# One channel tile at a time in the plain projections, and a third PSUM bank for neighbourhood outputs

## The chip, the core and the metric

The kernel runs on one core of a Trainium2 chip. The metric is device time in microseconds (us); lower is better. A core has a matrix engine (TensorE, PE in the profile, with its weight loads as PEld), VectorE (DVE), ScalarE (ACT), GpSimd (POOL) and SyncE (SP), which here issues nearly all DMA transfers, one after the other from one queue. [...] TensorE is throttled at times: the profile gives its granted clock, 1.00 being full speed.

## What is computed

One layer of an encoder over a prompt of 1024 tokens and a sample of 256, width 2048, then a final norm:

```python
hn = rmsnorm(x, norm_w)
proj = jnp.einsum('btd,dp->btp', hn, w_in)
cuts = [int(c) for c in np.cumsum([NA_WIDTH] * 4 + [2 * ML_WIDTH, ML_WIDTH, ML_WIDTH, ML_WIDTH])]
na_q, na_k, na_v, na_g, ml_qk, ml_v, ml_o, ml_z, ml_gp = jnp.split(proj, cuts, axis=-1)
...
att = (att * jax.nn.silu(na_g)).astype(x.dtype)
qk = jax.nn.silu(centred_depthwise_conv(ml_qk, conv_w, conv_b))
...
h = bidirectional_mlstm(mq, mk, mv, gates)
h = rmsnorm(h, head_norm_w.reshape(ML_HEADS, ML_HEAD_DIM)).reshape(B, T, ML_WIDTH)
mem = (h * jax.nn.sigmoid(ml_o.astype(f32)) * jax.nn.silu(ml_z.astype(f32))).astype(x.dtype)
mixed = jnp.concatenate([att, mem], axis=-1)
return x + jnp.einsum('btm,md->btd', mixed, w_out)
```

`att` is neighbourhood attention: 8 heads of width 128, each token attending to a window of 8 x 16 tokens in a grid 64 wide, with a learned bias. The mLSTM has 4 heads of width 256 and runs over chunks in both directions. The sample and the prompt are separate sequences. Everything is float32; the kernel splits each operand into a high and a low part and adds three products (high-high, high-low, low-high).

## The kernel before, in words

**Stages.** Channels of the projection come in tiles of 128, numbered from `QT0` (attention q), `KT0` (k), `GT0` (gates), `QK0` (the mLSTM's q and k, with a convolution), `OT0` and `ZT0` (its gates); v comes in units `u` of `proj_v`. First comes group A of the tokens (768 of the prompt), in `pair_a` with Strassen-like sums, to about 1097 us. Then group B (the last 256 of the prompt and the sample, 512 tokens): some pairs of tiles by `pair_s` (those in `SECOND`), the others plainly by `proj_pair` and `proj_v`. From about 1350 us attention and the mLSTM run beside these plain units, to about 2115 us; then the pairs of `late_gate`, and from 2160 us the output projection (`product`, L1613), with weights loaded from `w_o` into tiles `wr_wp` (pieces of 512 KB through the ring of `w_piece`), `wb` and `T`, split into `wo`.

**What sets the order.** All loops are unrolled by a planner that simulates the program and gives every engine a fixed order; each engine then waits on semaphores. The function `run` (L1304) issues two streams at high priority: the units of attention (`na_sample`, then `na_prompt` with its four blocks, for each of 8 heads) and those of the mLSTM (tiles `mls`, `mlp`). The plain projection units are of normal priority and fill TensorE where the streams cannot. DMAs go out of SP's queue in program order, each when its own waits are met, so a waiting DMA holds those behind it.

**PSUM.** `bank` (L73) gives a tile of one bank from one of two rings: `pr`, three banks, for the projections, and `a`, five banks, for everything else (scores, transposes, outputs of attention, the mLSTM's sums). `first_tiles`, `pair_a`, `pair_s` and the output projection (`p_banks`) take from both.

**`proj_pair` (L650).** A pair of channel tiles takes two `pr` banks. For each of four weight pieces (`w_piece`, 512 KB, a ring of two) it splits the columns of both tiles (`w_split`, ACT writes the high part at L165, DVE the low at L166), and goes through the four 128-column blocks of each split, for each of which the three products of the two tiles follow one another; 96 matmuls of 128 x 512 in all (`pc`, L662). Then both tiles are evicted (`out_scaled`, L251) and stored.

**`proj_v` (L709 on).** A unit of v takes two `pr` banks with two token tiles of 256 columns each (`pv`, L740), all four of which are evicted at the end by `store_v` (L221): ACT writes the high part (L168), DVE the low (L169) of a tile `vo`, which is stored to DRAM (`vS`).

**`na_sample` (L795) and `na_prompt` (L837).** Each loads q and k from DRAM (`qS`, `kS`), 2 x 256 KB for the sample and 2 x 1024 KB for the prompt, into a tile `qk` of tag `nqk`, which has one buffer. `na_softmax` computes scores into a bank `s` (L773) and the softmax, `na_transpose` the transposes (L790), and the products with v go to a bank `o` of ring `a`. The mLSTM's q, k, v tiles come from a ring `hf` of eight buffers.

**Square of the hidden state (L1258 to 1259).** Its value `jk` is not used, only its row sums; it goes into a ring `sml` of six small tiles.

## Time and profile before

| | us |
|---|---|
| median of 3 runs | 2563.29 |
| lowest, highest | 2563.03, 2566.54 |
| profiled execution | 2565.18 |
| its span | 2563.3 |

The mean granted clock of the profiled execution is 0.997. The page gives busy time, share of the span and number of instructions for each engine, and the chain of work that ended last, followed back from the last instruction. The rows of waits read: engine, what it ran next, its line, what released it; then total us, times and the longest one. A row of windows gives busy time of PE, PEld, DVE, ACT and POOL with the number of instructions, the granted clock, the DMA share and GB/s. In rows of a tile, three figures with slashes are the minimum, median and maximum duration in ns. Chain rows are start, duration, and what.

The span falls into these stages:

| us | stage |
|---|---|
| 7 to 1097 | projections of group A |
| 1097 to 1350 | first units of group B, pairs of `SECOND` |
| 1350 to 2115 | attention and mLSTM, plain units between |
| 2113 to 2153 | last pairs of `late_gate` |
| 2160 to 2554 | output projection |

### The profile page before, as it was taken

To read this page: it belongs to the slowest core of one execution; us is meant where nothing else is said; L and a number is where in the kernel's file an instruction comes from. 1 tells how busy PE (TensorE), PEld (TensorE's weight loads), DVE (VectorE), ACT (ScalarE), POOL (GpSimd) and SP (SyncE) were. 2 spreads that over 40 slices of the span, in tenths; PEclk is the share of its full clock that TensorE was granted. 3 is DMA by queue.
4 is the path that set the end of the run, shared out by engine and by line. 5 is a ranking of instruction groups with operands and counts; after the bars stand their busy time and mean duration, and the time that the engine had idled before them with its cause. 6 is when DMAs were issued, how large, how long until landed. Compare 5 with 4: busy or idle time off the path is not lost.

```text
span 2563.3 us, 44540 instructions
## 1 busy us (share of the span) xinstructions
PE 2534.0 (99%) x15054; PEld 2368.6 (92%) x15054; DVE 1972.6 (77%) x4029; ACT 1345.0 (52%) x3041; POOL 615.3 (24%) x909
## 2 busy tenths in 40 slices
PE   8999999999999999999999999999999999999998
PEld 8999999999999999999999999998988887788886
DVE  8769888888869798898875866765855665879695
ACT  8535545444444444465655666655745543344444
POOL 0535555444544444410001110100100104000001
PEclk9999999999999999999999999999999999999999
DMA  6546464536434342467768878877867849636237
GB/s 215 174 143 200 143 199 130 179 124 200 125 112 126 101 141 89 154 228 223 239 223 299 297 243 272 293 234 261 286 197 251 277 126 377 202 125 218 85 87 254
DMA packets 303483, 503.03 MB, mean 196 GB/s; under 512 B 48752, under 2 KB 191256, under 8 KB 303256
## 3 DMA queue, kind: packets, MB, share of 16 engines
q1 hardware_dynamic: 299096, 484.46, 58.9%
q0 software_dynamic: 4160, 15.73, 1.6%
q8 instruction: 119, 1.95, 0.3%
q14 instruction: 108, 0.88, 0.1%
HBM read 373.13 MB, written 126.95 MB: 195 GB/s over the span
## 4 chain that ended last, share of the span: by engine, by line
PE 92%; DMA 5%; DVE 2%; issue 1%; ACT 1%; SPq 0%; POOL 0%; ACTq 0%; POOLq 0%; DVEq 0%
PE pc L662 16%; PE po L1613 14%; PE pv L740 5%; PE fb L274 2%; PE A24b L274 1%; PE A12b L274 1%; PE A16b L274 1%; PE A44b L274 1%; PE A48b L274 1%; PE A52b L274 1%; PE A40b L274 1%; PE A20b L274 1%; PE A8b L274 1%; PE A50b L274 1%; PE A42b L274 1%; PE A22b L274 1%
## 5 line engine op out<-in xcount | busy, mean ns | idle before, releaser
L1613 PE MATMUL po<-wo,mo 128*128 128x512 f32 x1620 | 376.9, 393 | 3.7 <-ACT wo L165 2.8
L1613 PEld LDWEIGHTS po<-wo,mo 128*128 128x128 f32 x1620 | 303.6, 188 | 76.2 <-ACT wo L165 4.2
L166 DVE TENSOR_TENSOR ws<-wr,ws 128x512 fp32r<-128x512 f32 x152 | 104.3, 696 | 53.2 <-ACT ws L165 52.4
L165 ACT CAST ws<-wr 128x512 fp32r<-128x512 f32 x152 | 92.5, 617 | 70.1 <-PE pc L662 57.5
L165 ACT CAST mo<-mb 128x640 fp32r<-128x640 f32 x72 | 51.8, 726 | 92.5 <-PE po L1613 73.7
L116 POOL TENSOR_SCALAR rs<-rs 128x1 f32<-128x1 f32 x10 | 3.4, 341 | 351.2 <-DVE rs L1593 351.1
L166 DVE TENSOR_TENSOR mo<-mb,mo 128x640 fp32r<-128x640 f32 x72 | 59.1, 827 | 27.1 <-ACT mo L165 27.0
L1562 DVE TENSOR_TENSOR y<-y,po 128x512 f32<-128x512 f32 x90 | 58.5, 687 | 11.3 <-PE po L1613 11.0
L165 ACT CAST mo<-ms 128x640 fp32r<-128x640 f32 x40 | 28.9, 726 | 61.1 <-PE po L1613 32.1
L166 DVE TENSOR_TENSOR wsv<-wr_v,wsv 128x512 fp32r<-128x512 f32 x64 | 44.4, 700 | 14.2 <-ACT wsv L165 13.9
L165 ACT CAST wsv<-wr_v 128x512 fp32r<-128x512 f32 x64 | 39.0, 617 | 26.8 <-PE pv L740 15.5
L1576 ACT ACTIVATE jk<-y 128x512 f32<-128x512 f32 x40 | 25.2, 631 | 36.5 <-DVE y L1562 36.2
L413 DVE SCALAR_TENSOR_TENSOR pcv<-pco,cw_sb,pcv 128x516 f32<-128x516 f32 x48 | 36.7, 764 | 7.1 <-ACT pcv L407 7.0
L166 DVE TENSOR_TENSOR mo<-ms,mo 128x640 fp32r<-128x640 f32 x40 | 32.8, 823 | 7.6 <-ACT mo L165 7.6
L129 ACT ACTIVATE xq<-xq 128x1024 f32<-128x1024 f32 x20 | 21.2, 1061 | 31.7 <-DMA xq<-in_xtok_dram 29.2
L1081 POOL MEMSET mls_0v<- 128x2 f32 x4 | 0.4, 102 | 145.1 <-DVE S_dt.float L166 119.7
L274 PE MATMUL fb<-xg,fw 128*128 128x384 f32 x192 | 34.6, 334 | 0.0
L251 DVE TENSOR_TENSOR pco<-pc,rstdb 128x512 f32<-128x512 f32 x30 | 20.6, 687 | 17.8 <-PE pc L662 17.1
L274 PEld LDWEIGHTS fb<-xg,fw 128*128 128x128 f32 x192 | 33.4, 188 | 0.0
L778 DVE CUSTOM_DVE_ANT_0 nap_0st<-nap_0s,nap_0bt 128x384 f32<-128x384 f32 x32 | 17.7, 555 | 20.1 <-PE nap_0s L773 8.7
L1525 DVE TENSOR_TENSOR ms<-mb,mb 128x640 f32<-128x640 f32 x40 | 32.8, 823 | 0.0
L1492 POOL DMA_DIRECT2D mb<-mx x32 | 17.7, 554 | 58.8 <-DVE ws L166 24.8
(2655 smaller groups left out, 8512.4 us busy)
## 6 DMA issues: line engine op xcount, KB each, us to landing
wr<-in_w_in_dram SPq DMA_DIRECT2D x76, 512.0 KB, 4.7
wr_v<-in_w_in_dram SPq DMA_DIRECT2D x32, 512.0 KB, 5.0
wb<-in_w_o_dram SPq DMA_DIRECT2D x48, 256.0 KB, 3.0
xq<-in_xtok_dram SPq DMA_DIRECT2D x20, 512.0 KB, 4.2
mb<-mx POOLq DMA_DIRECT2D x32, 320.0 KB, 8.2
wr_wp<-in_w_o_dram SPq DMA_DIRECT2D x16, 512.0 KB, 4.0
vS<-vo SPq DMA_DIRECT2D x24, 256.0 KB, 5.1
nap_0bt<-in_rpb_tab_dram SPq DMA_DIRECT2D x32, 192.0 KB, 4.3
```

What stands on the lines that cost most here:

```text
L129: S.activation(raw, raw, AF.Square, accum_out=ssq[g][:, t, q : q + 1])
L165: S.copy(hi, src)
L166: V.tensor_tensor(lo, src, f(hi), op=ALU.subtract)
L251: V.tensor_tensor(o, src, rb, op=ALU.mult)
L274: PE.matmul(o, w(a_), x(b_), start=first and m == 0, stop=last and m == 2)
L413: V.scalar_tensor_tensor(dst[:, a:n], src[:, a + j - pad : n + j - pad], cw_sb[:, ct, j : j + 1], dst[:, a:n], op0=ALU.mult, op1=ALU.add,)
L662: PE.matmul(pb[j], t[j][:, wi, c : c + P], xs[xi], start=first and m == 0, stop=last and m == 2,)
L740: PE.matmul(outs[tt], xs[:, tt * P : (tt + 1) * P], t[:, wi, q * w : (q + 1) * w], start=first and m == 0 and (gates or tt % 2 == 0), stop ...
L1525: V.tensor_tensor(t, x, y_, op=op)
L1562: V.tensor_tensor(Y[p, q, tt], Y[p, q, tt], bk, op=op)
L1576: S.activation(jk, Y[p, q, tt], AF.Square, accum_out=ss[t][:, c : c + 1])
L1613: PE.matmul(bk[tt], m[xi][:, tt * P : (tt + 1) * P], w[wi], start=first and kk == 0 and j == 0, stop=last and j == 2, skip_group_check=True,)
```

## The change

1. PSUM has three rings: `pr` with two banks, `m` with one, `a` with five. Where three `pr` banks were taken at once (`first_tiles`, `pair_a`, `pair_s`, `p_banks`), the third is now `m`. The output banks `o` of `na_sample` and `na_prompt` move from `a` to `m`.
2. `proj_pair` does one channel tile after the other, each in a bank of its own, which is evicted as soon as it is complete. A weight piece now holds 512 columns of two blocks of rows, where before it held 1024 columns of one; there are as many pieces, splits and matmuls as before, and a piece's runs in DRAM are 2 KB instead of 4 KB.
3. In `proj_v`, `store_v` gets high priority.
4. `na_sample`'s q and k go to a tile of the ring `hf`; `nqk` is left to the prompt.
5. The ring `sml` has seven tiles, and the square's `jk` a tile of its own.

```diff
     def bank(tag, name):
-        return ps.tile([P, 512], F32, tag=tag, name=name, bufs=3 if tag == "pr" else 5)
+        return ps.tile([P, 512], F32, tag=tag, name=name, bufs={"pr": 2, "m": 1, "a": 5}[tag])
...
-        tags = ("pr", "pr", "pr", "a", "a", "a", "a")
+        tags = ("pr", "pr", "m", "a", "a", "a", "a")
...
     def proj_pair(n1, X, late=False):
-        pb = [bank("pr", f"pc{n1}_{j}") for j in range(2)]
-        for r in range(4):
-            raw = w_piece(w_in[n1 // 2, r], f"{n1}_{r}")
-            t = [w_split(raw, j * 512, j * 512 + 512, f"{n1}_{r}{j}") for j in range(2)]
-            for f_ in range(2):
-                for q in range(2):
-                    xs = X.get(8 * f_ + 2 * r + q)
-                    c = (2 * f_ + q) * P
-                    first, last = r + f_ + q == 0, r == 3 and f_ == 1 and q == 1
-                    for j, passes in enumerate((FORTH, FORTH[::-1])):
-                        for m, (wi, xi) in enumerate(passes):
-                            PE.matmul(
-                                pb[j], t[j][:, wi, c : c + P], xs[xi],
-                                start=first and m == 0, stop=last and m == 2,
-                            )
         out = []
         for j in range(2):
+            pb = bank("m" if n1 + j == QT0 else "pr", f"pc{n1}_{j}")
+            for r in range(4):
+                if r % 2 == 0:
+                    raw = w_piece(
+                        w_in[n1 // 2, r : r + 2, :, j * 512 : (j + 1) * 512].rearrange(
+                            "r p c -> p r c"
+                        ),
+                        f"{n1}_{j}{r}",
+                    )
+                t = w_split(raw, r % 2 * 512, r % 2 * 512 + 512, f"{n1}_{j}{r}")
+                for fq in range(4):
+                    f_, q = divmod(fq, 2)
+                    xs = X.get(8 * f_ + 2 * r + q)
+                    first, last = r + fq == 0, r + fq == 6
+                    for m, (wi, xi) in enumerate(FORTH[:: (1, -1)[fq % 2]]):
+                        PE.matmul(
+                            pb, t[:, wi, fq * P : fq * P + P], xs[xi],
+                            start=first and m == 0, stop=last and m == 2,
+                        )
             o = po(f"pco{n1}_{j}")
...
-            store_v(u, GA + tt * P, o, outs[tt][:, :256], rc[:, tt : tt + 1])
+            with tc.high_priority():
+                store_v(u, GA + tt * P, o, outs[tt][:, :256], rc[:, tt : tt + 1])
...
     def sml(name, n=256, dt=F32):
-        return ap.tile([P, 260], dt, tag="sml", name=name, bufs=6)[:, :n]
+        return ap.tile([P, 260], dt, tag="sml", name=name, bufs=7)[:, :n]
...
     def na_sample(h):
         nm = f"nas{h}"
-        qk = na_tile("nqk", [P, 4, TP], f"{nm}qk", 1, F32R)[:, :, :TS]
+        qk = hf(f"{nm}qk")[:, : 4 * TS].rearrange("p (i c) -> p i c", i=4)
...
-        b = bank("a", f"{nm}o")
+        b = bank("m", f"{nm}o")
...
-            b = bank("a", f"{n2}o")
+            b = bank("m", f"{n2}o")
...
-                jk = sml(f"{n2}jk{e}")
+                jk = ap.tile([P, 256], F32, tag="jk", name=f"{n2}jk{e}", bufs=1)
...
-    def pair_s(n1, tag, bg):
+    def pair_s(n1, tags, bg):
...
-        bx, by, bz = (bank(tag, f"{nm}b{i}") for i in "xyz")
+        bx, by, bz = (bank(t, f"{nm}b{i}") for t, i in zip(tags, "xyz"))
...
-        bg = pair_s(n, ("pr", "a")[i % 2], bg)
+        bg = pair_s(n, (("pr", "pr", "m"), ("a", "a", "a"))[i % 2], bg)
...
-    slots = iter(("aaaaa" "ppp") * 8)
+    slots = iter((("a",) * 5 + ("pr", "pr", "m")) * 8)
```

More of the change, by code (lines that the diff above doesn't have):

```diff
@@ L282, in first_tiles @@
     def first_tiles():
-        names = ("pr", "pr", "pr", "a", "a", "a", "a", "a")
+        names = ("pr", "pr", "m", "a", "a", "a", "a", "a")
         pb = [bank(t, f"fb{j}")[:, :HALF] for j, t in enumerate(names)]
@@ L675, in proj_pair @@
                     o[:, 4:].rearrange("p (s c) -> p s c", s=2)[:, :, :256],
-                    pb[j].rearrange("p (s c) -> p s c", s=2),
+                    pb.rearrange("p (s c) -> p s c", s=2),
                     rbs[1].rearrange("p (s c) -> p s c", s=2), n1,
@@ L682, in proj_pair @@
             o = o[:, :GB]
-            out_scaled(o, pb[j], rbs[1], n1)
+            out_scaled(o, pb, rbs[1], n1)
             if n1 < GT0:
@@ L1644, in product @@
             each(tt)
-    slots = iter(("aaaaa" "ppp") * 8)
+    slots = iter((("a",) * 5 + ("pr", "pr", "m")) * 8)
     def p_banks(p, j):
-        return [bank("pr" if next(slots) == "p" else "a", f"po{p}_{j}_{i}") for i in range(NT)]
+        return [bank(next(slots), f"po{p}_{j}_{i}") for i in range(NT)]
     for i in range(4):
```

## The prediction

> **What bounds the kernel now.** I read the page first, then the waits of TensorE, then the windows around them, then the DMA rows. The page:
>
> ```profile
> PE 2534.0 (99%) x15054; PEld 2368.6 (92%) x15054; DVE 1972.6 (77%) x4029; ACT 1345.0 (52%) x3041; POOL 615.3 (24%) x909
> PE 92%; DMA 5%; DVE 2%; issue 1%; ACT 1%; SPq 0%; POOL 0%; ACTq 0%; POOLq 0%; DVEq 0%
> PE pc L662 16%; PE po L1613 14%; PE pv L740 5%; PE fb L274 2%; PE A24b L274 1%; PE A12b L274 1%; PE A16b L274 1%; PE A44b L274 1%; PE A48b L274 1%; PE A52b L274 1%; PE A40b L274 1%; PE A20b L274 1%; PE A8b L274 1%; PE A50b L274 1%; PE A42b L274 1%; PE A22b L274 1%
> ```
>
> TensorE is busy 99% of the span and is most of the chain that ended last. What an edit can save is therefore TensorE's idle time, and time in which it runs slowly. All its waits:
>
> ```profile
> PE fb L274 <- ACT fw L172: 7.1, 1, 7.1
> PE po L1613 <- ACT wo L165: 2.8, 2, 1.8
> PE nap_0s L773 <- DMA nap3qk<-kS: 2.5, 1, 2.5
> PE nap_0s L773 <- DMA nap4qk<-kS: 1.9, 1, 1.9
> PE A4b L274 <- DVE A4s L173: 1.7, 1, 1.7
> PE A6b L274 <- ACT A4c L483: 1.5, 1, 1.5
> PE po L1613 <- DVE wo L166: 0.8, 2, 0.5
> PE mgpmc L987 <- DVE mgprm L981: 0.6, 1, 0.6
> PE nap_0s L773 <- DMA nap2qk<-kS: 0.5, 1, 0.5
> ```
>
> The first is the start of the kernel, which the change leaves alone. The prompt's scores (`nap_0s`) wait for their k three times, 2.5 + 1.9 + 0.5 = 4.9 us. The output projection (`po`) waits 2.8 + 0.8 = 3.6 us for split weights, all of it at its beginning. A4 and A6 are early, in the first group of tokens. The windows show a second price of the two longer waits (busy time and, in brackets, instructions of PE, PEld, DVE, ACT, POOL; then granted clock, DMA share, GB/s):
>
> ```profile
> 1632.25:1635.66 3.41, 1.28 (x8) 1.27 (x9) 1.09 (x3) 0.49 (x1) 0.32 (x1) 1.00 1.05 385
> 1635.66:1639.07 3.41, 3.41 (x19) 3.41 (x17) 3.24 (x10) 1.95 (x6) 1.77 (x6) 0.50 1.07 391
> 1639.10:1642.50 3.40, 3.40 (x29) 3.40 (x28) 2.28 (x9) 2.45 (x6) 0.00 (x0) 1.00 0.62 209
> 1731.24:1734.65 3.41, 1.55 (x12) 1.38 (x11) 1.02 (x4) 1.64 (x5) 0.89 (x2) 1.00 1.03 340
> 1734.65:1738.06 3.41, 3.41 (x17) 3.41 (x16) 2.59 (x9) 1.23 (x4) 0.00 (x0) 0.50 1.03 376
> 1738.10:1741.50 3.40, 3.40 (x31) 3.40 (x31) 1.48 (x5) 3.08 (x8) 0.00 (x0) 1.00 0.85 262
> 2164.68:2168.09 3.41, 2.42 (x11) 1.63 (x9) 0.78 (x2) 0.72 (x1) 1.30 (x4) 1.00 1.03 390
> 2168.09:2171.50 3.41, 2.57 (x11) 2.12 (x12) 3.12 (x5) 2.18 (x4) 1.93 (x4) 1.00 1.03 386
> ```
>
> A window in which TensorE was busy 1.28 or 1.55 us is followed by one at granted clock 0.50, with 19 and 17 matmuls where the next has 29 and 31. Half of each slow window is lost: 2 x 3.41 / 2 = 3.4 us. After 2.42 us busy (the wait of `po`, last two rows) the clock stayed at 1.00.
>
> The Trainium skill ("TensorE: Matmul & The Clock Gate", section "Why this matters for your kernels") has the clock halve after one whole window of idle, and asks only that no gap exceed about 3 us. The rows disagree: gaps of 2.5 and 1.9 us, in windows with 1.28 and 1.55 us of work, were enough, and the measurement decides. By the page's rule the 3.4 us would not hang on these waits and would stay.
>
> **The change part by part.** Numbers called cover below are the matmul time that stands, in the order of the two built programs, between what starts a piece of work and the matmul that needs it; matmuls count at the rate of rows like this one:
>
> ```profile
> 2202.00:2302.00 100.00, 100.00 (x434) 81.27 (x434) 82.36 (x126) 39.24 (x68) 0.00 (x0) 1.00 0.46 141
> 1097.30:1105.60 8.30, 8.30 (x69) 8.30 (x68) 7.39 (x15) 3.28 (x6) 0.91 (x5) 1.00 0.69 224
> ```
>
> that is 100/434 = 0.230 us for 512 columns and 8.30/69 = 0.120 us for 256. Both programs issue the same matmuls, so the 2534 us of work costs the same.
>
> *Prompt q and k (the sample's pair leaves the shared tile `nqk`).* `nqk` has one buffer. Before, the prompt's 2 MB can be asked for only when the sample's scores, in the same buffer, are done:
>
> ```profile
> L773 PE MATMUL nas_1s<-nas3qk x3: 274/277/279, 1619.5 to 1619.7; 128*128 128x256 f32 x3
> L844 SPq DMA_DIRECT2D nap3qk<-qS x1: 524/524/524, 1623.4 to 1623.4; - x1
> L845 SPq DMA_DIRECT2D nap3qk<-kS x1: 602/602/602, 1624.0 to 1624.0; - x1
> 1624.02 10.22 DMA nap3qk<-kS
> 1723.24 10.59 DMA nap4qk<-kS
> ```
>
> The sample's last score began at 1619.7, the k load was issued at 1624.0 and came 10.22 us later, 14.5 us in all; the cover in the order was 11.0 to 11.8 us for heads 1 to 7. With a tile of the mLSTM ring for the sample, the prompt's load waits for the previous head's prompt scores alone, and its cover becomes 22.7 (head 4) to 62 us. That exceeds 14.5 by 8 us everywhere: gain 4.9 us of waits and the 3.4 us of slow windows, 8.3 us. The clock part is nothing or all: bounds 4.9 to 8.3.
>
> *The sample's own q and k (2 x 256 KB).* On SP's queue they now come behind the next head's 2 MB in odd heads. Cover is 16.1 us (head 1), 17.3 (3), 16.3 (5), 14.0 (7), and 12.3 to 14.3 in heads 2, 4, 6, 0. Before, nothing lay ahead of them:
>
> ```profile
> DMA to landing us min/median/max: 3.3/3.3/3.3
> 1300.00:1900.00 600.00, 594.89 (x4096) 553.06 (x4095) 420.72 (x1117) 363.41 (x898) 53.30 (x208) 0.99 0.82 264
> ```
>
> (the first row is head 5's.) Behind 2 MB they land at the latest after the prompt's 10.6 plus their own 3.3 plus 1.6 of issue = 15.5 us; that eats the cover of head 7 and leaves 0.6 to 1.8 us on heads 1, 3, 5. At the full traffic of the second row, 0.264 MB/us, the 2.5 to 3.5 MB that stand ahead of and in them take 10 to 13 us, with 2 to 4 us of fixed time 12 to 17. I take 0.8 us in all; bounds 0 and 5.5 (14 to 17.3 us of cover each short by about 1.4 on four heads).
>
> *Two banks for the pairs, one tile at a time, and priority for v's stores.* Within a pair, the eviction of the first tile now runs under the second tile's 48 matmuls (48 x 0.230 = 11 us), and that costs nothing. What loses cover is a pair's first tile after a v unit (`proj_v`): v holds both banks, where before a third was free. Its first bank comes free after two halves, each an ACT and then a DVE pass:
>
> ```profile
> L168 ACT ACTIVATE vo<-pv,rstdc x4: 460/473/491, 1670.2 to 1675.3; 128x256 fp32r<-128x256 f32 x4
> L169 DVE SCALAR_TENSOR_TENSOR vo<-pv,rstdc,vo x4: 481/483/484, 1670.7 to 1677.1; 128x256 fp32r<-128x256 f32 x4
> ```
>
> Four passes are 2 x (0.473 + 0.483) = 1.9 us, 2.3 with hand-overs. The cover is v's second bank, 12 x 0.120 = 1.4 us, where nothing else fits in between: at 1667 and 1844 of the order; it is 1.9 at 1729 and at least 3.7 elsewhere, and before it was 5.1 or more. Short by 0.9 + 0.9 + 0.4 = 2.2, which I take. Lower bound 1 (ACT works ahead of DVE: three passes). Upper: before, the four halves took 1670.2 to 1677.6, 7.4 us, as other work came between; half of that less 1.4 is 2.3, on three places 6, which high priority should prevent: 5.
>
> *Beginning of attention.* As pairs now end tile by tile, the unit that used to fill TensorE between the first mLSTM steps is used up sooner. Five groups of matmuls at 1358 to 1364 of the order, with 2.9 us of cover or more before, have 0.0 (the first k-v product behind ACT's weighting of k), 1.2 to 1.8, and 1.9 to 2.1. Before there was no wait here:
>
> ```profile
> 1350.00:1365.00 15.00, 15.00 (x130) 15.00 (x129) 7.41 (x17) 6.15 (x15) 2.08 (x13) 1.00 0.99 313
> ```
>
> The first needs a copy and a weighting, two passes near the 0.473 us above with two hand-overs, 1.1 us; the later ones lack some 0.6. I take 1.7. Bounds 0.5 (the weighting alone) and 5 (2.9 lost in full on the first, 2.1 on the `hs` chain behind it).
>
> *Transition to the output projection.* The wait of 1.8 us came behind 4 MB of other weights:
>
> ```profile
> 2153.34 12.37 DMA T<-in_w_o_dram
> 2165.76 15.80 DMA wr_wp<-in_w_o_dram
> ```
>
> The pair's weight pieces end sooner, and two `wr_wp` pieces are now issued ahead of the `T` tiles; the covers of their splits go from 0.0, 1.4 and 3.5 us to 9.7, 10.2 and 10.4. This takes the 1.8 and 0.6 of the small ones: 2.4, perhaps 0.5 more. Bounds 0 (the queue is as full, DMA share 1.03 above) and 3.6.
>
> *Small edits.* Weight pieces keep 512 KB but have runs half as long. The nearest rows:
>
> ```profile
> wr<-in_w_in_dram SPq DMA_DIRECT2D x76, 512.0 KB, 4.7
> wb<-in_w_o_dram SPq DMA_DIRECT2D x48, 256.0 KB, 3.0
> ```
>
> Two of the second kind, whose runs have that half length, are 6.0 against 4.7 us, hidden by a ring that is loaded one piece (24 matmuls, 5.5 us) ahead; uncovered it would be 1.3 a piece. Bank m, the own tile for the square, and the seventh small buffer only remove waits of ACT and DVE, which are not on the path; I put 0.2 us of loss for one new cover of 2.1 at 100 of the order (before, A6 waited 1.5 near there) and the like; bounds -1 and 2.
>
> **Sum.** -4.9 - 3.4 - 2.4 - 0.5 + 0.8 + 2.2 + 1.7 + 0.2 = -6.3 us. The profiled execution took 2565.18 us around its span of 2563.3, so 2558.9; it stands 1.9 above the median of 2563.29, so against the median 2557.0. The best ends give -11.9 - 1 + 1.5 = -11.4 (2552), the worst -4.9 + 5.5 + 5 + 5 + 2 = +12.6.
>
> **The rivals.**
> 1. *Given back.* Bank waits and the first mLSTM steps both at 5 us: -11.2 + 5 + 5 + 0.8 + 0.2 = -0.2, 2563.1. For it: v's evictions took 7.4 us; against: the priority and DVE's 77%.
> 2. *Slower: the sample's loads become the wait.* If they land after more than their 12.3 to 17.3 us of cover, heads wait there instead. Each wait of 2.5 us with its slow window costs 2.5 + 1.7 = 4.2; on five heads 21, with 11.2 gained and 4.1 lost elsewhere: +13.9, 2577.2; on three +5.5, 2568.8. It decides from three heads. For it: 15.5 us at the latest; against: 264 GB/s on average leaves room, and the 2 MB now start earlier, not more of them.
> 3. *Clock not recovered.* Some other wait still falls in a window and the slow windows stay: -6.3 + 3.4 = -2.9, 2560.4. The windows' rows speak against it.
>
> By the Trainium skill's rule ("TensorE: Matmul & The Clock Gate", section as above) rival 3 is what follows for gaps of this length.
> 4. *The change doesn't do what it says.* The prompt's load stays held, by another tile or by SP's queue: -6.3 + 8.3 = +2.0, 2565.3. Against: the covers of 22.7 us and more.
>
> **How the numbers follow.** Forecast 0.55, rivals 0.15, 0.12, 0.12, 0.06. 0.2% of 2563.29 is 5.1 us, about what a measurement of this kernel tells from no change, so faster begins below 2558.2, inside the forecast's own range of 2552 to 2562. Of its 0.55, 0.38 goes to faster, as its middle lies there, and 0.17 to same. Rivals 1, 3 and 4 are mostly same: of their 0.33, 0.04 is faster and 0.05 slower. Rival 2 is slower. That gives faster 0.42, same 0.41, slower 0.17. The range goes to 2569, which takes in rivals 1, 3 and 4 and rival 2 on up to three heads, and from 2551, the sum's best ends less one.
>
> **What would show it.** Right: no `nap_0s` row waiting on a `nap` load, no granted clock of 0.50 past 1100 us, `po` waiting under 1.5 us; new small rows of `pc` behind DVE's vo and of the first mLSTM products behind ACT. Wrong: rows of `nas_0s` or `nas_1s` behind a `nas` load (rival 2), `pc` behind vo above 5 us together (rival 1), 0.50 windows kept (3), the nap rows kept (4).

## The result, and the profile after

The changed kernel is slower. Its median is 2569.1 us (8 runs, 2565.63 to 2575.43), that of the kernel before, on the same chip and in turn with it, 2562.3 us (8 runs, 2559.49 to 2566.54). The ratio is 1.0027, interval 1.0017 to 1.0038, or +6.8 us, where 2557.0 was forecast. The profiled execution of the changed kernel took 2571.18 us around a span of 2569.5. That of the kernel before (2565.18) turns out to stand 2.9 us above the median of its eight runs.

Of the page of the changed kernel, the row of busy time and the chain that ended last by engine:

```profile
PE 2535.3 (99%) x15054; PEld 2367.8 (92%) x15054; DVE 1966.1 (77%) x4029; ACT 1340.6 (52%) x3041; POOL 613.0 (24%) x909
PE 84%; DMA 7%; DVE 5%; issue 1%; ACT 1%; SPq 0%; POOL 0%; ACTq 0%; POOLq 0%; DVEq 0%
```

The matmuls are as many as before, and TensorE is still busy 99% of the span. PE's share of the chain fell from 92% to 84%, about 200 us of the span, while TensorE's waits beside attention grew by 6 us (4.9 to 11.0): that share is no measure of the loss. The waits of TensorE (what ran next, what released it; total us, times, longest):

```profile
PE mls_0s L1100 <- DMA mls_0q<-cS: 2.1, 1, 2.1
...
PE mlp0a3kv L1100 <- issue: 1.6, 1, 1.6
PE pc L668 <- DVE vo L169: 1.6, 2, 0.8
PE mls_0s L1100 <- issue: 1.4, 1, 1.4
PE po L1619 <- DVE wo L166: 1.3, 1, 1.3
PE nas_0s L778 <- DMA nas2qk<-qS: 1.3, 1, 1.3
...
PE po L1619 <- DVE y L1568: 0.9, 1, 0.9
...
PE mlp_2s L1100 <- DVE nap_0sm L783: 0.8, 1, 0.8
PE nap_0o L891 <- issue: 0.7, 1, 0.7
PE mlp_3tp L1271 <- DVE mlp_3hs L1269: 0.5, 1, 0.5
```

The prompt's waits for k (`nap3qk`, `nap4qk`, `nap2qk`) are gone, as forecast. In their place stand the waits that were forecast (`pc` behind vo, `mlp0a3kv`, `nas2qk`) and others that were not: `mls_0s`, the mLSTM's scores of the sample, 2.1 + 1.4 us, and a row of 0.5 to 0.8 us each on products of the streams.

To see where the time went without going by single waits, three marks that both programs share will do: the first mLSTM score, the first matmul of the output projection (all matmuls of the pairs come ahead of it in both) and the end. Between the first two marks lie the same number of matmuls in both programs. A second execution of each kernel was profiled later. First and last start are the two figures with "to" between them; before, its second execution, after, its second execution:

```profile
L1095 PE MATMUL mls_0s<-mls_0q,mls_0k x48: 278/282/334, 1360.3 to 1891.3; 128*128 128x256 f32 x48
L1613 PE MATMUL po<-wo,mo x1620: 387/393/506, 2160.0 to 2550.7; 128*128 128x512 f32 x180
```

```profile
L1095 PE MATMUL mls_0s<-mls_0q,mls_0k x48: 278/282/385, 1361.1 to 1889.2; 128*128 128x256 f32 x48
L1613 PE MATMUL po<-wo,mo x1620: 386/393/498, 2157.9 to 2549.7; 128*128 128x512 f32 x180
```

```profile
L1100 PE MATMUL mls_0s<-mls_0q,mls_0k x48: 278/283/550, 1361.6 to 1869.8; 128*128 128x256 f32 x48
L1619 PE MATMUL po<-wo,mo x1620: 387/393/503, 2168.5 to 2556.9; 128*128 128x512 f32 x180
```

```profile
L1100 PE MATMUL mls_0s<-mls_0q,mls_0k x48: 279/283/357, 1361.3 to 1867.1; 128*128 128x256 f32 x48
L1619 PE MATMUL po<-wo,mo x1620: 387/393/503, 2165.9 to 2553.7; 128*128 128x512 f32 x180
```

| us | first mLSTM score | from there to the first `po` | from there to the end | span |
|---|---|---|---|---|
| before | 1360.3 | 799.7 | 403.3 | 2563.3 |
| before, second | 1361.1 | 796.8 | 404.4 | 2562.3 |
| after | 1361.6 | 806.9 | 401.0 | 2569.5 |
| after, second | 1361.3 | 804.6 | 400.3 | 2566.2 |
| change of the mean | +0.8 | +7.5 | -3.2 | +5.1 |

The output projection gained 3.2 us. The stretch in the middle, called the attention stage below, lost 7.5 us, where the forecast's terms for it add up to -3.6 (-4.9 - 3.4 + 0.8 + 2.2 + 1.7). The experiments are about that stage.

### The profile page after: what moved, and what is told of

Read it like the earlier page. It is cut to its first block, busy times and chain, and to the rows that moved or that the text cites. A ratio compares the mean times of both kernels' runs of the same rounds, so it can differ in the third digit from the quotient of the medians.

```text
span 2569.5 us, 44539 instructions
## 1 busy us (share of the span) xinstructions
PE 2535.3 (99%) x15054; PEld 2367.8 (92%) x15054; DVE 1966.1 (77%) x4029; ACT 1340.6 (52%) x3041; POOL 613.0 (24%) x909
## 4 chain that ended last, share of the span: by engine, by line
PE 84%; DMA 7%; DVE 5%; issue 1%; ACT 1%; SPq 0%; POOL 0%; ACTq 0%; POOLq 0%; DVEq 0%
PE pc L668 14%; PE po L1619 11%; PE pv L744 5%; PE fb L274 2%; PE A24b L274 1%; PE A12b L274 1%; PE A44b L274 1%; PE A20b L274 1%; PE A48b L274 1%; PE A16b L274 1%; PE A40b L274 1%; PE A52b L274 1%; PE A8b L274 1%; PE A50b L274 1%; PE A42b L274 1%
```

## The experiments

Each kernel ran with the kernel before on the same chip, whose median was between 2561.4 and 2562.4 us in the five groups. "Attention" is the length of the attention stage in the one profiled execution (before: 799.7 and 796.8), and "waits" the sum of TensorE's waits from 1350 to 2115 us there (before: 4.9 and 3.9; after: 11.0 and 10.0). Parts are numbered as in the section on the change.

| kernel | median us (runs) | against before | ratio, interval | attention | waits |
|---|---|---|---|---|---|
| part 4 alone | 2568.28 (6) | +6.2 | 1.0027, 1.0016 to 1.0038 | 801.1 | 7.7 |
| part 2 alone | 2561.14 (11) | -1.2 | 0.9994, 0.9985 to 1.0003 | 796.4 | 2.9 |
| part 5 alone | 2560.16 (11) | -2.2 | 0.9992, 0.9984 to 1.0001 | 794.9 | 2.3 |
| parts 2, 3, 5 | 2559.74 (11) | -1.7 | 0.9996, 0.9988 to 1.0005 | 795.3 | 4.0 |
| part 1 alone | 2596.37 (4) | +34 | 1.0132, 1.0118 to 1.0146 | 818.5 | 18.0 |
| all but part 4 | 2567.7 (11) | +5.6 | 1.0017, 1.0008 to 1.0026 | 803.4 | 7.9 |
| all but part 1 | 2569.09 (8) | +7.0 | 1.0026, 1.0017 to 1.0036 | 802.2 | 7.4 |

**Part 4 alone: the sample's q and k in the ring `hf`.**

```diff
-        qk = na_tile("nqk", [P, 4, TP], f"{nm}qk", 1, F32R)[:, :, :TS]
+        qk = hf(f"{nm}qk")[:, : 4 * TS].rearrange("p (i c) -> p i c", i=4)
```

> The kernel before with the change's fourth part alone (the sample's q and k in the mLSTM ring). Theory A (the new waits for the mLSTM's q come from the two pr banks): the prompt's scores wait no more and no window falls to clock 0.50 (-8.3 us), the first mLSTM products wait as in the changed kernel (+2.2 us), no wait of mls_0s for its q; 4 to 8 us faster than before. Theory B (the load edit itself lets the streams run into their data): mls_0s waits 3.7 us in all with a slow window (1.7 us) and nas2's scores 1.3; within 2 us of before.

Measured: +6.2 us, which neither theory had. The waits on the `nap` loads are gone here too, and the kernel is as slow as the full change. TensorE waits elsewhere, longest in `mlp_2s`, 5.3 us in three places. Around the longest of them, the timeline of DVE in this kernel (start, us, line, operation; in brackets the idle time before it and what ended it), and PE's next row:

```profile
1482.45 0.42 DVE L1279 SCALAR_TENSOR_TENSOR mlp_0zr<-mlp_0or,mlp_0zr 128x256 f32<-128x256 f32 x1 [2.35 <-DMA mlp_0zr<-pT]
1482.79 0.41 DVE L1194 TENSOR_TENSOR mlp_2d<-mlp_2d,mlp_2s 128x256 f32<-128x256 f32 x1
1483.12 0.47 DVE L1280 SCALAR_TENSOR_TENSOR mlp_0zr<-mlp_0tp,w_sb,mlp_0zr 128x256 f32<-128x256 f32 x1
```

```profile
1483.74 1.33 PE L1095 MATMUL mlp_2s<-mlp_2q,mlp_2k 128*128 128x256 f32 x6 [2.25 <-DVE mlp_0zr L1280]
```

DVE sat idle 2.35 us for a 128 KB gate tile of the mLSTM (`mlp_0zr`). DVE runs in the planner's fixed order, so `mlp_2d`, which does not name that tile, came only behind it, and TensorE after them waited 2.25 us. So a small load that is late for one block holds the work of another, through the fixed order of an engine that is not the bound. The other 3.1 us of `mlp_2s` follow DVE's `nap_0pt` and are not traced to a load.

**Part 2 alone, and part 5 alone.** Part 2's diff is the one of `proj_pair` above, with three `pr` banks; part 5's:

```diff
-        return ap.tile([P, 260], dt, tag="sml", name=name, bufs=6)[:, :n]
+        return ap.tile([P, 260], dt, tag="sml", name=name, bufs=7)[:, :n]
...
-                jk = sml(f"{n2}jk{e}")
+                jk = ap.tile([P, 256], F32, tag="jk", name=f"{n2}jk{e}", bufs=1)
```

> The kernel before with the pairs done one tile at a time (second part alone, three pr banks). Theory F (what lets the streams of attention and mLSTM run ahead of the plain units turns the waits for the prompt's k into waits for small loads, and costs 4 to 7 us; this part doesn't let them): within 2 us of before, the wait of po at the transition gone (-2 to -3). Theory N (the order of before is a favourable one, and any other order costs some 5 us): 3 to 7 us slower.

> The kernel before with the fifth part alone (seven sml tiles, the square's tile of its own). Theory F: 0 to 3 us faster than before, as the loads of the mLSTM's gate tiles go out sooner. Theory N: 3 to 7 us slower, through the order alone.

Measured: -1.2 and -2.2 us, both with 1.0 inside the interval. The planner gives both programs an order of their own, as it does the full change, so a new order is not in itself a loss. The wait of the first mLSTM products (`mlp0a3kv`), which the prediction put down to part 2, does not occur in either.

**Parts 2, 3 and 5.** From the changed kernel, with three `pr` banks and no `m`, and the sample's pair back in `nqk`:

```diff
-        return ps.tile([P, 512], F32, tag=tag, name=name, bufs={"pr": 2, "m": 1, "a": 5}[tag])
+        return ps.tile([P, 512], F32, tag=tag, name=name, bufs={"pr": 3, "a": 5}[tag])
...
-            pb = bank("m" if n1 + j == QT0 else "pr", f"pc{n1}_{j}")
+            pb = bank("pr", f"pc{n1}_{j}")
...
-        qk = hf(f"{nm}qk")[:, : 4 * TS].rearrange("p (i c) -> p i c", i=4)
+        qk = na_tile("nqk", [P, 4, TP], f"{nm}qk", 1, F32R)[:, :, :TS]
...
-        b = bank("m", f"{nm}o")
+        b = bank("a", f"{nm}o")
```

> The kernel before with the pairs by tiles, v's priority, and the small rings (second, third and fifth part; three pr banks, one q-k tile). Both theories: no stream is let ahead; each of the two main parts alone stood 1.2 to 2.2 us below before, so together 2 to 4 us faster than before, 2558 to 2561. If the parts don't add up: 2561 to 2563.

Measured: -1.7 us, with an interval that includes 1.0. So these three parts together show no loss (part 3 was not run by itself), and the loss lies with parts 1 and 4. It is not their sum.

**All but part 4, and all but part 1.** The edits are those of the last diff, one half each.

> The changed kernel with its fourth part undone (sample and prompt share the one q-k tile again). Theory A: mls_0s still waits for its q (2 to 4 us), pc still waits for v's eviction (about 1.6), the prompt's scores wait again (3 to 6 us, with up to two slow windows), the 2.2 us of the first mLSTM products go: 0 to 6 us slower than the changed kernel. Theory B: no wait of mls_0s, the prompt's waits are back: as before, or up to 3 us slower than before.

> The changed kernel with three pr banks and no bank m (outputs of attention back in ring a); loads, pairs by tiles and the rest as changed. Theory A: pc no longer waits for v's eviction (-1.6 to -1.9 us), mls_0s waits under 1 us and no window falls to 0.50 (-5 us); the first mLSTM products still wait 2.2 us; 6 to 11 us faster than the changed kernel. Theory B: mls_0s still waits 3 us or more; 1 to 3 us faster than the changed kernel.

Measured: +5.6 and +7.0 us; the full change is +6.8. Against parts 2, 3 and 5 alone, each of the two costs 7 to 9 us (5.6 + 1.7 = 7.3; 7.0 + 1.7 = 8.7), and having both costs no more than either. All but part 1, waits of TensorE in the attention stage:

```profile
PE mlp0a3kv L1100 <- issue: 1.7, 1, 1.7
PE nap_2o L900 <- ACT nap_2os L897: 1.2, 1, 1.2
```

The waits of `pc` behind vo and of `mls_0s` on its q have gone with the third `pr` bank; others of about 1 us stand in their place, and the time is the same. Without part 4 it is `mlp_3tp` 2.2, `mlp_3in` 1.9 and `pc` 1.6 us, and two windows at clock 0.50. So the wait of `pc` belongs to part 1. That of `mls_0s` on its q needs parts 1 and 4 together: without part 4 that row is 0.2 us. Neither theory of these two experiments had a time that came out.

**Part 1 alone, and the variant without `m`.** First the kernel before with two `pr` banks and `m`, the pairs as before; then all but part 4 with two `pr`, six `a` and no `m`:

```diff
-        return ps.tile([P, 512], F32, tag=tag, name=name, bufs=3 if tag == "pr" else 5)
+        return ps.tile([P, 512], F32, tag=tag, name=name, bufs={"pr": 2, "m": 1, "a": 5}[tag])
...
-        b = bank("a", f"{nm}o")
+        b = bank("m", f"{nm}o")
```

```diff
-        return ps.tile([P, 512], F32, tag=tag, name=name, bufs={"pr": 2, "m": 1, "a": 5}[tag])
+        return ps.tile([P, 512], F32, tag=tag, name=name, bufs={"pr": 2, "a": 6}[tag])
...
-            pb = bank("m" if n1 + j == QT0 else "pr", f"pc{n1}_{j}")
+            pb = bank("a" if n1 + j == QT0 else "pr", f"pc{n1}_{j}")
```

> The kernel before with the banks alone (two pr, one m for the outputs of attention; pairs still take both pr banks at once). Theory F: the plain pairs wait for banks (pc and pv behind DVE's eviction, about 0.7 to 1.3 us at some eight places), 4 to 9 us slower. Theory N: 3 to 7 us slower as well, but without those waits as its main rows.

> The changed kernel without the load edit, with two pr banks and six of ring a (no bank m; outputs of attention in a). If the banks cost time because plain pairs start late behind v's eviction and the mLSTM's q then comes late: pc waits for vo (0.8 to 2 us twice), mls_0s waits 1 to 4 us for its q (cover 8.2 us for head 2), 2566 to 2571. If the single bank m for the outputs was the cost: 2559 to 2563.

Measured: 2596.37 us (+34) and 2593.93 us (+31.7; 1.0119, 1.0105 to 1.0133). In the first, the attention stage takes 818.5 us and the first mLSTM score comes 9.8 us later than before. That a pair holding both `pr` banks leaves none for the next unit is only part of it: `pc` behind vo is 1.6 us of the 18.0 us of waits there, and the largest row is the mLSTM's `mlp_1in` behind ACT, 8.9 us. In the second it is the gates of the mLSTM, far ahead of attention, whose banks are all in ring `a` (the windows: total, busy time of PE, PEld, DVE, ACT and POOL with counts, granted clock, DMA share, GB/s):

```profile
1152.40:1180.00 27.60, 10.66 (x48) 8.19 (x49) 19.05 (x92) 9.57 (x19) 0.00 (x0) 0.57 0.40 135
```

TensorE did 10.66 us of work in 27.60, at a mean clock of 0.57; the first mLSTM score starts at 1385.2 instead of 1361.6, and the attention stage itself takes 800.8. How the bank rings bring these stalls about was not followed further; both kernels are slower by far more than either expectation had.

**Head 0's early prompt load.** All but part 1, with head 0's sample pair left in `nqk`:

```diff
+        qk = (
+            hf(f"{nm}qk")[:, : 4 * TS].rearrange("p (i c) -> p i c", i=4) if h
+            else na_tile("nqk", [P, 4, TP], f"{nm}qk", 1, F32R)[:, :, :TS]
+        )
```

> As the last one (three pr banks), and the sample of head 0 alone stays in the q-k tile that it shares with the prompt, so that head 0's 2 MB are not asked for ahead of the first mLSTM tiles. Theory A, with the wait of the first mLSTM products put down to those 2 MB in SP's queue: that wait (1.6 to 2.2 us) goes as well; 8 to 13 us faster than the changed kernel, 3 to 7 faster than before. If that wait comes from the pairs' new order instead (as the prediction had it), it stays, and the time is that of the last one.

Measured: 2566.06 us (12 runs), +4.0 (1.0016, 1.0007 to 1.0026), 3.0 less than with head 0 treated like the others, though the two intervals overlap; the wait on `mlp0a3kv` is gone, and the gain of 8 to 13 us did not come. In the kernel before and in the changed kernel, the issue of head 0's prompt load (SPq) and the weighting of k that the first k-v product needs (ACT; first and last start):

```profile
L844 SPq DMA_DIRECT2D nap0qk<-qS x1: 524/524/524, 1370.9 to 1370.9; - x1
L1066 SPq DMA_DIRECT2D mlp0a3cv<-cD x2: 332/332/332, 1363.7 to 1365.0; - x2
L168 ACT ACTIVATE mlp0a3w<-mlp0a3tb,mgpw x2: 474/474/474, 1372.3 to 1373.3; 128x256 fp32r<-128x256 f32 x2
```

```profile
L849 SPq DMA_DIRECT2D nap0qk<-qS x1: 530/530/530, 1358.2 to 1358.2; - x1
L1071 SPq DMA_DIRECT2D mlp0a3cv<-cD x2: 320/822/1323, 1364.6 to 1367.1; - x2
L168 ACT ACTIVATE mlp0a3w<-mlp0a3tb,mgpw x2: 474/474/475, 1377.4 to 1378.5; 128x256 fp32r<-128x256 f32 x2
```

Free of the sample, the 2 MB go out 12.7 us earlier and now lie ahead of the small convolution tile `mlp0a3cv`; the weighting comes 5 us later. The wait occurs in every kernel in which head 0's pair has left `nqk`, with or without part 2 (0.6 to 1.7 us), and in none in which its k stays there.

**The other ring, and the hold kept.** Three more kernels on the base "all but part 1": the pair in the ring `nv` of attention's v tiles instead of `hf`; the same with head 0 left in `nqk`; and only q in `hf`, with k left in `nqk`, so that the prompt's load is held as before.

```diff
+        qk = na_tile("nv", [P, 4, 2, P], f"{nm}qk", NV, F32R).rearrange("p i z d -> p i (z d)")
```

```diff
+        qt = hf(f"{nm}q")[:, : 2 * TS].rearrange("p (i c) -> p i c", i=2)
+        kt = na_tile("nqk", [P, 4, TP], f"{nm}k", 1, F32R)[:, :2, :TS]
```

> As the experiment with three pr banks, but the sample's q and k lie in the ring of attention's v tiles (three tiles of the same size) instead of the mLSTM ring. If letting the 2 MB go early is the cost: 2565 to 2570 again, with the wait of the first mLSTM products (1.1 to 1.8). If sharing the mLSTM ring is: 2559 to 2563.

> As the experiment with the other ring (pairs by tiles, small rings, three pr banks), and the sample of head 0 stays in the tile shared with the prompt: the wait of the first mLSTM products (1.6 us) goes, the rest of attention waits under 2 us; 2558 to 2561, faster than before by 1 to 4 us. If new waits come with the changed start, 2562 to 2565.

> As the experiment with three pr banks, but only the sample's q lies in the mLSTM ring; its k stays in the tile that it shares with the prompt, so the prompt's 2 MB are held until the sample's scores as before. If what the load edit costs (some 8 us between the experiment with three pr banks and the one with pairs and rings) comes from letting the 2 MB and the streams go early: 2558 to 2562, PE's waits in attention back to 3 to 5 us, the first mLSTM products without a wait. If it comes from sharing the mLSTM ring: 2565 to 2569, waits as there.

| parts 2, 3, 5 and | median us (runs) | against before | ratio, interval | attention | waits |
|---|---|---|---|---|---|
| pair in `hf` | 2569.09 (8) | +7.0 | 1.0026, 1.0017 to 1.0036 | 802.2 | 7.4 |
| in `hf`, head 0 in `nqk` | 2566.06 (12) | +4.0 | 1.0016, 1.0007 to 1.0026 | 802.4 | 6.9 |
| pair in `nv` | 2562.22 (11) | 0.0 | 0.9997, 0.9988 to 1.0006 | 792.4 | 2.0 |
| in `nv`, head 0 in `nqk` | 2559.21 (11) | -2.4 | 0.9993, 0.9984 to 1.0001 | 793.1 | 1.6 |
| q in `hf`, k in `nqk` | 2559.04 (11) | -3.2 | 0.9988, 0.9980 to 0.9997 | 796.0 | 3.2 |

The first four form a square: by the medians head 0 is worth 3.0 and 2.4 us, with intervals that overlap, and the ring 7.0 and 6.4 us, with intervals that do not. The last one is the only kernel of this study whose interval lies below 1.0. Its upper end is 0.9997, and with this many kernels compared one such interval can be chance; that it is faster than the full change is clear. Its waits in the attention stage begin with

```profile
PE nap_0s L778 <- DMA nap3qk<-kS: 1.5, 1, 1.5
...
PE nap_0s L778 <- DMA nap4qk<-kS: 0.8, 1, 0.8
```

which are the very waits that the change was to remove. With the whole pair in `hf` they are gone and the time is 10 us longer; with the pair in `nv` they are gone too and nothing of that size came in their place.

**Does the ring decide by itself?** The kernel before, with the pair in `nv` and nothing else:

> The kernel before with the sample's q and k in the ring of attention's v tiles, and nothing else: the same release of the prompt's load as in the first experiment, with a plan that differs little from it, but without a share in the mLSTM ring. If the shared mLSTM ring is what costs: the waits of mlp_2s behind DVE (5.3 us) and their slow window go, 2559 to 2563. If letting the 2 MB go early is: 2566 to 2570, with waits like those of the first experiment.

Measured: 2569.3 us (6 runs), +7.7 (1.0030, 1.0018 to 1.0042), the same as part 4 alone in `hf` (+6.2). So "share the other ring" does not carry over to another base, and the ring is not shown to be a cause by itself.

**Three theories that fell.** That the late gate tiles of the first experiment are the price: the kernel before with part 4 and without the loads of the mLSTM's output gates and their product (its output leaves out `sigmoid(ml_o) * silu(ml_z)`). That part 5 gives DVE and ACT the room they lack: part 4 and part 5 together. That the q pair of the mLSTM, which now ends late, is the price: the changed kernel with the plain units in another order,

```diff
-        for u in (("v", 4 + i), QK0 + 8 + 2 * i, QK0 + 2 * i, ("v", i), QT0 + 2 * i, KT0 + 2 * i):
+        for u in (QK0 + 8 + 2 * i, QK0 + 2 * i, ("v", 4 + i), ("v", i), QT0 + 2 * i, KT0 + 2 * i):
```

> The first experiment (the sample's q and k in the mLSTM ring) with the two gate loads of the mLSTM's output left out, and with them their product: the output tile is only scaled. Theory F, with DVE's in-order wait for these loads (14.2 us of DVE's idle time there) as what holds TensorE at the second mLSTM block of a head: the waits of mlp_2s (5.3 us) and the slow window (1.7) go; 5 to 9 us faster than that experiment. If these loads aren't the cause, within 2 us of it.

> The first experiment with the fifth part added (load edit, seven sml tiles, the square's own tile). Theory G (with six tiles, two of them taken by the square, the gate loads of the mLSTM's output get their tiles late; DVE waits for them in order and holds TensorE): DVE's waits for mlp_0zr fall from 14.2 us to under 7, the waits of mlp_2s (5.3 us) and their slow window (1.7) go, the first mLSTM products still wait 2.2 us; 3 to 7 us faster than the first experiment, 2562 to 2565. Theory F, the streams simply run ahead into the next late load: within 2 us of the first experiment.

> The changed kernel with the plain units of a head in another order: the mLSTM's k and q pairs ahead of its v, so that q is stored earlier (cover of mls_0q 15.8 and 15.9 us instead of 12.2). If the late q is one of the new waits: mls_0s waits under 0.5 us instead of 1.9 to 3.5, 2 to 5 us faster than the changed kernel (2564 to 2567), still slower than before. If other loads take its place: within 2 us of the changed kernel.

Measured: 2573.47 us (+11.1; 1.0047, 1.0034 to 1.0059), 2573.73 us (+12.3; 1.0051, 1.0037 to 1.0064) and 2567.3 us (+5.1; 1.0017, 1.0008 to 1.0026). The first two were expected to gain 3 to 9 us on part 4 alone, and are 5 to 6 us slower than it. Without the mLSTM's gate loads the same kind of wait came back behind a gate tile of attention, the first row below of TensorE, the second of DVE; here a late load of one stream does hold the other's product:

```profile
PE mlp_1in L1095 <- DVE nas1ot L833: 2.8, 1, 2.8
DVE nas1ot L833 <- DMA nas1ot<-pT: 3.6, 1, 3.6
```

With the units re-ordered the wait of `mls_0s` fell from 3.5 to 0.9 us, and `nas1o` and `nas0o` took 2.7 us in its place.

**The two kernels once more,** one profiled execution each:

> The kernel before once more, for a second profile. If the profile of before was an unlucky execution (2565.2 against a median of 2562.2 by now): the waits of nap_0s for k come to 0 to 3 us instead of 4.9 and at most one window falls to 0.50; 2560 to 2563. If it was typical: 4 to 6 us of waits and two slow windows.

> The changed kernel once more. If the cover of 12.2 us that the order leaves for mls_0q of heads 2 and 3 is what fails, both waits come again (1 to 2.5 us each, with or without a slow window), as do pc behind v's eviction (0.8 twice) and the first mLSTM products (1.5 to 2.3). If they are chance, at least one of the two mls_0s waits is missing and others stand in their place.

The kernel before, second execution (2564.2 us), in the attention stage:

```profile
PE nap_0s L773 <- DMA nap3qk<-kS: 1.9, 1, 1.9
...
PE mls_0s L1095 <- DVE mls_0d L1194: 0.8, 1, 0.8
PE mlp_1in L1095 <- DVE nap_0pt L793: 0.7, 1, 0.7
PE nap_0s L773 <- DMA nap2qk<-kS: 0.5, 1, 0.5
```

The wait on `nap4qk` is not there, and only one window ran at 0.50. The changed kernel, second execution (2567.93 us), had none at 0.50; `mls_0s` waited 1.4 + 0.5 us, `nas2qk` 1.3, `pc` behind vo 1.6, `mlp0a3kv` 1.1. So the small waits of the changed kernel repeat, and half of what it was to gain was there in one of the two executions of the kernel before and not in the other.

## Why the prediction was wrong, point by point

The attention stage, from the waits of the two executions of each kernel (means; a 0.50 window counts 1.7 us):

| us | forecast | found | how |
|---|---|---|---|
| prompt's waits for k | -4.9 | -3.6 | before 4.9 and 2.4, after none |
| windows at 0.50 | -3.4 | -1.7 | before two and one, after one and none |
| sample's own loads | +0.8 | +1.3 | `nas2qk` 1.3 and 1.3 |
| `pc` behind vo | +2.2 | +1.6 | 1.6 and 1.6, on two places |
| first mLSTM products | +1.7 | +1.3 | `mlp0a3kv` 1.6 and 1.1 |
| mLSTM's scores of the sample | - | +2.3 | after 3.5 and 1.9, before 0 and 0.8 |
| other waits of 0.2 to 1.2 | - | +3.2 | after 3.0 and 4.1, before 0 and 0.7 |
| not in any wait | - | +3.1 | the rest to +7.5 |

The last row can be followed one step. Of TensorE between the first two marks, before, before again, after, after again:

```profile
1360.30:2160.00 799.70, 794.59 (x4945) 715.03 (x4943) 533.80 (x1425) 461.03 (x1134) 88.14 (x280) 1.00 0.79 260
1361.10:2157.90 796.80, 792.82 (x4945) 713.69 (x4945) 534.36 (x1425) 460.75 (x1134) 87.61 (x279) 1.00 0.79 261
1361.60:2168.50 806.90, 795.75 (x4944) 714.34 (x4943) 524.84 (x1427) 457.97 (x1134) 89.13 (x285) 1.00 0.79 259
1361.30:2165.90 804.60, 794.61 (x4945) 713.16 (x4944) 524.83 (x1427) 458.05 (x1134) 88.18 (x285) 1.00 0.79 260
```

Less 1.7 us for each window at 0.50, TensorE was busy 791.2 and 791.1 us before, 794.0 and 794.6 after. So the 3.1 us are in TensorE's busy time: the same matmuls took longer by the profile, which models their ends. What lengthened them stays open.

- *The prompt's q and k:* right in mechanism: no `nap_0s` row waits on a `nap` load any more. The size was read from one execution that was 2.9 us above its median; its 8.3 us were 4.1 in the next (2.4 + 1.7).
- *The sample's own loads:* +1.3 where 0.8 was put, on one head. The load `nas2qk<-qS` was issued at 1528.9 behind 1 MB of the prompt's, 8.1 us ahead of its score at 1537.0; before, it was issued at 1528.7 and its score came at 1541.5. Rival 2 named the place, but on one head, and it did not decide.
- *`pc` behind vo:* right (in the rows of `vo`, ACT and DVE carry v out of its PSUM banks, and `pc` takes one of these next), two places at 0.8 us, and the third `pr` bank takes it away.
- *Beginning of attention:* right in size, wrong in cause. It is not part 2 that makes it but head 0's prompt load, which part 4 lets out 12.7 us earlier.
- *Transition to the output projection:* -3.2 where -2.9 was forecast. `po` waits 1.3 us for split weights instead of 3.6; its wait of 0.9 behind `y` also stands in the second execution of the kernel before, with 1.0.
- *The rivals:* what rival 1 priced at 10 us (bank waits and first mLSTM steps) came to 2.9; rival 4 is out, the prompt's loads are free. The loss came by a way that none of the four names.
- *The clock:* rival 3 came in part, as one window at 0.50 in one of two executions:

```profile
1679.44:1682.85 3.41, 1.31 (x12) 1.18 (x11) 1.81 (x4) 0.58 (x3) 0.00 (x0) 1.00 1.02 339
1682.86:1686.27 3.41, 3.41 (x16) 3.41 (x17) 2.70 (x7) 1.18 (x3) 1.11 (x8) 0.50 0.37 124
```

The step that failed is "Small edits", with its 0.2 us "for one new cover of 2.1 at 100 of the order ... and the like". It left out the mLSTM's own loads, and with them everything that the new order does to the two streams: the waits that no term of the sum names came to 5.5 us (2.3 + 3.2). A second step failed beside it, "Both programs issue the same matmuls, so the 2534 us of work costs the same": in the attention stage it cost 3.1 us more. And the gain on the prompt's k, with its two slow windows, was taken at 8.3 us from one execution, where the means of two executions of each kernel give 5.3.

The clearest of the new waits can be read at head 2, in the rows of the sample's mLSTM q: when SP issues its load, how long it takes to land, and when the scores that need it run. Before, and after:

```profile
L1095 PE MATMUL mls_0s<-mls_0q,mls_0k x6: 281/283/283, 1709.8 to 1710.4; 128*128 128x256 f32 x6
L1072 SPq DMA_DIRECT2D mls_0q<-cS x1: 571/571/571, 1685.1 to 1685.1; - x1
DMA to landing us min/median/max: 4.9/4.9/4.9
```

```profile
L1100 PE MATMUL mls_0s<-mls_0q,mls_0k x12: 415/415/550, 1682.9 to 1685.3; 128*128 128x256 f32 x12
L1077 SPq DMA_DIRECT2D mls_0q<-cS x1: 529/529/529, 1677.3 to 1677.3; - x1
DMA to landing us min/median/max: 5.4/5.4/5.4
```

From the issue of the load to the first score it was 24.7 us and is 5.6. The transfer takes about as long as before; it is asked for late against its scores, because the plain pair that makes this q now ends later and its scores come earlier. The last stores of that q, before and after:

```profile
1660.78 0.91 SPq L243 DMA_DIRECT2D cS<-pco  x2
```

```profile
1671.95 0.88 SPq L243 DMA_DIRECT2D cS<-pco  x2
```

From the stores to the first score it was 49 us and is 11. After the change 5.4 us of that go from the store to the load and another 5.4 from the load to its landing at 1682.7, and the score ran at 1682.86 after a wait of 2.1 us and ahead of the slow window shown above. Where the pair and the scores stand could be read from the order of the two programs before the run. With three `pr` banks the wait is gone.

The other wait of `mls_0s`, 1.4 us at the last head, is not for q. That load was issued at 1860.5 and landed 4.2 us later, 2.1 us before the score. The rows ahead of the score, in the changed kernel, are again a late gate tile on DVE:

```profile
1865.39 0.42 DVE L1284 SCALAR_TENSOR_TENSOR mlp_2zr<-mlp_2or,mlp_2zr 128x256 f32<-128x256 f32 x1 [2.90 <-DMA mlp_2zr<-pT]
1866.78 0.95 PE L1100 MATMUL mls_0s<-mls_0q,mls_0k 128*128 128x256 f32 x6 [1.38 <-issue]
```

The profile names no releaser for this wait; that it hung on that tile is likely, but not shown.

Taking away the wait on q, or that of `pc`, did not bring the time back, and taking away the wait of the first products brought back 3 us at most, by the medians. What separates the runs is the length of the attention stage as a whole: 792 to 797 us in the variants that are no slower than before, 801 to 809 in all that are (leaving aside the two of +32 and +34 us). In the first group TensorE waits 1.6 to 4.0 us in that stage, in the second 6.7 to 13.2, in up to a dozen places that differ from kernel to kernel. These are figures of one execution of each kernel, some of them far from the median (2556.36 us against 2562.22 for the pair in `nv`), and the first execution of the kernel before, 799.7 and 4.9, lies between the groups. The streams of attention and of the mLSTM share DVE, ACT and POOL in one fixed order, and a small load that comes a microsecond or two late stops all that stands behind it, as `mlp_0zr`, `nas1ot` and `mlp_2zr` did. The forecast took that fabric of small covers as unchanged.

The cause of the loss is thus shown as to its place, the attention stage, and for single waits. What stays open: why parts 1 and 4, each alone on top of 2, 3 and 5, push the plan into the slower group, why the ring `nv` does not do so on that base and does on the kernel before, and why both parts together cost no more than one. Each variant gets its own order for 44539 instructions, and one kernel for each is not enough to tell a mechanism of the ring from the luck of an order. Most expectations of the experiments with the pair in a ring or with two `pr` banks named two theories, and in more than half of these neither gave the time that came.

## What to carry to other kernels

When two latency-bound streams share in-order engines beside a saturated TensorE, list the cover of every small load in the new order, not only of those that the edit names; a load that is freed to go early is a load ahead of others in the same queue. A wait of 2 us that the profile shows can be worth less than it looks if it is read from one execution: profile twice, and compare by stage between marks that both programs share. Split a bundle into its parts before keeping it: here three of five parts together cost nothing that can be seen, and keeping the hold on the prompt's k while moving only the sample's q (2559.04 us) is 10 us faster than the bundle, and perhaps 3 faster than the kernel before.

## What the runs showed of the hardware that was not expected

The granted clock follows fixed windows of 3.41 us, and the rule by which it halves is sharper than the prediction's two cases. Over the twenty profiled executions of this study, up to the last matmuls of each, every window at full clock in which TensorE was busy for at most 1.55 us (twenty of them) was followed by one at 0.50, and no window with 1.67 us or more ever was; between 1.56 and 1.62 us two were and one was not. The limit is thus near 1.6 of 3.41 us, a little under half. The way back has another limit: a window at 0.50 with 2.82 us of work or more was followed by full clock in each case, and one with 2.49 us or less by another at 0.50, so that a slow stretch can last several windows (10.2 us at 1152 us with part 1 alone). The second execution of the changed kernel shows the other side of the first limit, at the same place as the slow window above:

```profile
1681.10:1684.50 3.40, 1.98 (x17) 1.87 (x16) 1.80 (x6) 1.77 (x5) 1.10 (x8) 1.00 0.81 274
1684.50:1687.90 3.40, 3.21 (x29) 3.04 (x28) 3.40 (x11) 0.72 (x3) 0.00 (x0) 1.00 0.41 118
```

Its wait was 1.4 instead of 2.1 us, 1.98 us of work were left in the window, and the clock stayed. Whether a wait of 2 us costs 1.7 us more therefore hangs on how it falls on the windows, which differed between these two executions. The Trainium skill ("TensorE: Matmul & The Clock Gate", section "Why this matters for your kernels") has a window of idle and gaps of more than about 3 us as the condition. The runs here show that less is enough: gaps of 1.9 to 2.5 us were followed by a window at 0.50.

The weight pieces with runs of 2 KB instead of 4 KB cost nothing that can be seen: the queue's share of the engines' span was 58.9% before and 59.0% in the changed kernel, and part 2 alone was not slower.
